# Low parts of the weights on VectorE, paired delta-net products, and the sink attention's value products in one group

## The chip, the cores and the metric

One core of one Trainium2 chip runs the whole program. The metric is the time of one execution on the device in microseconds (us); the figure for a kernel is the median of its runs. TensorE (PE in the profile) multiplies matrices, VectorE (DVE), ScalarE (ACT) and GpSimd (POOL) do the elementwise work, and SyncE (SP) issues the DMAs.

## The reference

Two layers of a bidirectional encoder over 512 tokens of width 1024, all in float32. What matters of a layer:

```
h = rms_norm(x); split(h @ w_in) -> na q,k,v | swa q,k,v | delta net q,k,v,z,beta,a | gates
y_na  = neighborhood_attention_2d(...)       # 4 heads, softmax over a window
y_swa = sliding_window_gqa(..., sink)        # 8 q heads, 2 kv heads, 128-token blocks
y_gdn = gated_deltanet_bidir(...)            # 4 heads, both directions, chunks of 64
  lower = tril(k_beta @ k.T * decay, -1);  u, w = solve(lower + I, ...)
  per chunk:  v_new = u - w @ S;  S = S * d + k_tail.T @ v_new
merged = sum_i sigmoid(gate_i) * (y_i @ w_branch_i);  x = x + merged @ w_out
h = rms_norm(x); u = conv3(h @ w_up) + b;  x = x + (silu(a) * b) @ w_down
```

## The kernel before

Features lie on the 128 partitions and the 512 tokens along the free dimension, so an activation is eight tiles of 128x512. A dense product of 1024 inputs into 128 outputs is one *chunk* of weights, 128 chunks a layer, numbered by the constants at the head of the file: 0 to 51 feed the three mixers and their gates, 52 to 59 (`CH_OUT`) the output projection, 60 to 103 (`CH_UP`) the up projection, 104 to 127 (`CH_DN`) the down projection. `load_w` fetches a chunk in halves of 128x512. For each half it rounds the weights on ScalarE (line 142, the tile `hi`) and subtracts the rounded from the raw on GpSimd (line 144, the tile `lo`, the low parts). Three buffers each hold `raw`, `hi` and `lo`. `mm3` makes a product from three: high weights with high and with low activations (lines 150, 151), low weights with high activations (line 152).

Inside a layer the order of the steps is in the string `ORDER`: projections and attentions of the sliding window (`sp`, `sa`) and of the neighbourhood (`np`, `na`), then the delta net: gates, projections, `gdn_cross` (`gx`), `gdn_z`, `gdn_solve` (`gs`), `gdn_mid`, `gdn_scan` (`gc`), `gdn_out`, and the merges `mn`, `ms`, `mg`. This is only the order in which the program writes its instructions. When it is built, a scheduler orders each engine's list by a simulated timeline and by the tiles' buffers, so that dense products of later steps stand between the small ones of the delta net and of the attentions. On the chip each engine goes through its list in order. `tc.issue_after(i)` puts an order edge behind instruction `i` for what the block writes on the same engine.

`swa_attend` goes over two pairs of heads and four token blocks of 128. A block has two or three key blocks: for each, four transposes of the probabilities (line 531) into a bank `pt`, a copy to SBUF on ScalarE (tile `th`, through line 80) and, for both kv heads, a product with v (line 535) into halves of 64 columns of the bank `py`. A float32 product is two instructions in the profile.

`gdn_cross` makes, head by head, the decays and the masked products k·k and q·k of the chunks. A head's k and q lie on partitions 0 to 63 or 64 to 127 (`rr`), so its products (line 677) use 64 rows of the array. `gdn_solve` inverts the triangular matrices on VectorE in 31 steps (lines 713 and 715). `gdn_scan` goes over eight chunks in both directions at once: direction `d` uses the 64x64 tile of the array at (64d, 64d), with four heads each, for the products with the state (line 832) and for the state's update (line 843). `gdn_mid` has products of the same shape in which the two tiles alternate (line 812).

Of the kernel before, what the change touches and what calls it, by code (L numbers as in the profile page):

```python
# [61 lines left out]
def encoder_kernel(ctx, tc, xT, wall, par, cst, nab, out, depth=2, dbg=None):  # L62
# [70 lines left out]
    def load_w(l, c, nk=8):  # L133
        if (l, c) in early:
            return early.pop((l, c))
        ws = []
        for o in range(0, nk, 4):
            n = min(4, nk - o)
            raw = wp.tile([128, 4, 128], F32, tag="raw", name=nm("wr"), bufs=NB["raw"])
            lastw[0] = nc.sync.dma_start(out=raw[:, :n], in_=wall[l, c, :, o * 128:(o + n) * 128].rearrange("p (k m) -> p k m", k=n))  # L140
            hi = wp.tile([128, 4, 128], F32R, tag="hi", name=nm("wh"), bufs=NB["hi"])
            S.activation(out=hi[:, :n], in_=raw[:, :n], func=AF.Copy)  # L142
            lo = wp.tile([128, 4, 128], F32R, tag="lo", name=nm("wl"), bufs=NB["lo"])
            G.tensor_tensor(lo[:, :n], raw[:, :n], hi.bitcast(F32)[:, :n], op=ALU.subtract)  # L144
            ws += [(hi[:, k], lo[:, k]) for k in range(n)]
        return ws

# [88 lines left out]
    def n8(a):  # L236
        return a.rearrange("p (n i) -> p n i", n=8)
# [37 lines left out]
    for l in range(depth):  # L275
# [215 lines left out]
        def swa_attend():  # L491
            line[0] = "a"

            y["s"] = [None] * 4
            for ep in range(2):
                yh, yl = (big(F32R, (128, 2, 512), name=n) for n in ("ysh", "ysl"))
                for e in range(2):
                    y["s"][2 * ep + e] = (yh[:, e], yl[:, e])
                for b in range(4):
                    kb0, kb1 = max(0, b - 1), min(4, b + 2)  # L500
                    w = 128 * (kb1 - kb0)
                    pr_ = [None] * 4
                    for e in range(2):
                        c0 = 8 * b + 4 * ep + 2 * e
                        mx, sk = small(2, "s", 8), slice(4 * ep + 2 * e, 4 * ep + 2 * e + 2)
                        for gq in range(2):
                            sc = bank("at")
                            q_, kc = qs[2 * ep + e][gq][:, 128 * b:128 * b + 128], slice(128 * kb0, 128 * kb1)
                            T.matmul(sc[:, 0:w], lhsT=q_, rhs=kdh[gq][:, kc], start=True, stop=False)  # L509
                            T.matmul(sc[:, 0:w], lhsT=q_, rhs=kdl[gq][:, kc], start=False, stop=True)  # L510

                            pr = tmp(name="spr")
                            V.tensor_tensor_reduce(out=pr[:, 0:w], in0=sc[:, 0:w], in1=smask[:, 128 * (b == 0):128 * (b == 0) + w], scale=rqs[:, c0 + gq:c0 + gq + 1],
                                                   scalar=nsink[:, sk.start + gq:sk.start + gq + 1], op0=ALU.add, op1=ALU.min, accum_out=mx[:, gq:gq + 1])
                            pr_[2 * gq + e] = pr
                        es, rs = small(2, "s", 8), small(2, "s", 8)
                        V.tensor_tensor(es, mx, P[:, P_SK + sk.start:P_SK + sk.stop], op=ALU.add)
                        S.activation(out=es, in_=es, func=AF.Exp)
                        for gq in range(2):
                            pr = pr_[2 * gq + e]  # L520
                            S.activation(out=pr[:, 0:w], in_=pr[:, 0:w], func=AF.Exp, bias=mx[:, gq:gq + 1], scale=-1.0, accum_out=rs[:, gq:gq + 1])
                        V.tensor_tensor(rs, rs, es, op=ALU.add)
                        V.reciprocal(rs, rs)
                        for gq in range(2):
                            on("spr", "V").tensor_scalar(pr_[2 * gq + e][:, 0:w], pr_[2 * gq + e][:, 0:w], rs[:, gq:gq + 1], None, op0=ALU.mult)
                    py = bank("at")
                    for kb in range(kb0, kb1):
                        pt = bank("at")
                        c0 = 128 * (kb - kb0)
                        for i in range(4):  # L530
                            T.transpose(pt[:, 128 * i:128 * i + 128], pr_[i][:, c0:c0 + 128], ident)  # L531
                        pT = tmp(name="th")
                        copy("th", pT, pt)
                        for gq in range(2):
                            T.matmul(py[64 * gq:64 * gq + 64, 0:256], lhsT=vst[:, 128 * kb + 64 * gq:128 * kb + 64 * gq + 64],  # L535
                                     rhs=pT[:, 256 * gq:256 * gq + 256], start=kb == kb0, stop=kb == kb1 - 1, tile_position=(0, 64 * gq))
                    bs = slice(128 * b, 128 * b + 128)
                    pyv = py[:, 0:256].rearrange("p (e t) -> p e t", e=2)
                    S.activation(out=yh[:, :, bs], in_=pyv, func=AF.Copy)
                    V.tensor_tensor(yl[:, :, bs], pyv, yh.bitcast(F32)[:, :, bs], op=ALU.subtract)  # L540
# [109 lines left out]
        def gdn_cross():  # L650
# [4 lines left out]
            Xo, Xg, Lt = (big(F32, (128, 32, 32), name=n) for n in ("Xo", "Xg", "Lt"))  # L655
            kds = [[doubled(kq[j][i][:, :, 0, :]) for i in range(2)] for j in range(2)]
            qdec = pair(name="qd") + pair(name="qd")
            for hh in range(4):
                j, rr = hh // 2, slice(64 * (hh % 2), 64 * (hh % 2) + 64)
                pe, pr = decay_sums(hh, (msr, blk))  # L660
                eg = tmp(name="eg")
                S.activation(out=eg, in_=pr, func=AF.Exp)
                for d in range(2):
                    r = slice(64 * d, 64 * d + 64)
                    for i in range(2):
                        ns = slice(4 * i, 4 * i + 4)
                        V.tensor_tensor(n8(qdec[hh])[r, ns], n8(eg)[r, ns], kq[j][i][rr, :, 1, :], op=ALU.mult)  # L667
                T.matmul(pe, lhsT=idb, rhs=nmb.unsqueeze(1).to_broadcast([128, 8, 64]), start=False, stop=True)
                e = tmp(name="E")
                S.activation(out=e, in_=pe, func=AF.Exp)  # L670
                on("ebk", "V").tensor_tensor(n8(e), n8(e), bc(bk, hh, 0, 8), op=ALU.mult)
                xt = tmp(name="X")
                for n0 in (0, 4):
                    kd = kds[j][n0 // 4]
                    pk = bank("gd")
                    for n in range(4):
                        T.matmul(pk[:, 128 * n:128 * n + 128], lhsT=kd[rr, n].rearrange("p d i -> p (d i)"),
                                 rhs=kq[j][n0 // 4][rr, n].rearrange("p c i -> p (c i)"), start=True, stop=True)
                    pkv = pk.rearrange("p (n c i) -> p c n i", n=4, c=2)
                    en = n8(e)[:, n0:n0 + 4]  # L680
                    V.tensor_tensor(n8(xt)[:, n0:n0 + 4], pkv[:, 0], en, op=ALU.mult)
                    V.tensor_tensor(Qu[n0 // 4 * 2 + hh // 2][:, :, hh % 2], pkv[:, 1], en, op=ALU.mult)

                for q4 in range(4):
                    r = slice(32 * q4, 32 * q4 + 32)
                    o = 32 * (q4 % 2)
                    cpx = (S.activation if q4 % 2 else G.tensor_copy)(
                        out=Xg[r].rearrange("p i (h n) -> p h n i", h=4)[:, hh], in_=n8(xt)[r, :, o:o + 32], **({"func": AF.Copy} if q4 % 2 else {}))
                    if q4 == 2:
                        lastg[0] = cpx  # L690
                    if q4 in (0, 3):
                        S.activation(out=Xo[r, 8 * hh:8 * hh + 8], in_=n8(xt)[r, :, 32 - o:64 - o], func=AF.Copy)
            Rt = big(F32, (128, 32, 32), "Rt")

        def gdn_solve():
# [121 lines left out]
        def gdn_scan():  # L817
# [7 lines left out]
            for s in range(8):  # L825
                ns = (s, 7 - s)
                half = [slice(0, 64), slice(64, 128)]
                if s:
                    pv = bank("gd", (128, 4, 64))
                    for d, r in enumerate(half):  # L830
                        for hh in range(4):
                            T.matmul(pv[r, hh], lhsT=n8(wn[hh])[r, ns[d]], rhs=SA(ns[d])[r, hh], start=True, stop=True,  # L832
                                     tile_position=(64 * d, 64 * d))
                    for d, r in enumerate(half):
                        V.tensor_tensor(VN(ns[d])[r], pv[r], VN(ns[d])[r], op=ALU.add)
                if s < 7:
                    pd = bank("gd", (128, 4, 64))
                    sd = tmp(shape=(128, 8, 64), name="sd")[:, 0:4]
                    for d, r in enumerate(half):
                        if s:  # L840
                            G.tensor_tensor(sd[r], SA(ns[d])[r], hn(dec[:, 64:96])[r, :, ns[d]].unsqueeze(2).to_broadcast([64, 4, 64]), op=ALU.mult)
                        for hh in range(4):
                            T.matmul(pd[r, hh], lhsT=kT(ns[d], hh)[r], rhs=VN(ns[d])[r, hh], start=True, stop=True,  # L843
                                     tile_position=(64 * d, 64 * d))
                    for d, r in enumerate(half):
# [286 lines left out]
```

## Time and profile before

| what | value |
|---|---|
| median of 3 runs | 1711.9 us (1708.8 to 1712.89) |
| the profiled execution | 1711.75 us, span 1710.0 us |
| mean granted TensorE clock | 0.986 |
| busy TensorE | 1656.6 us (97%) |
| busy VectorE | 1008.1 us (59%) |
| busy GpSimd | 834.5 us (49%), of it line 144 683.8 us in 512 instructions of 1344 ns |
| busy ScalarE | 739.1 us (43%) |
| the chain that ended last | TensorE 79%, VectorE 14% |

Busy is the union of an engine's instructions; matmuls overlap, so their steps are read from start to start. In the timeline a row may merge neighbouring instructions of one line ("x16"), and the time from its start to the next row's start is what the run takes. The two layers lie at 0 to about 860 us and from there to the end; in each the mixers come first, then the two projections of the feed-forward part.

### The profile page before, as it was taken

To read this page: it belongs to the slowest core of one execution; us is meant where nothing else is said; L and a number is where in the kernel's file an instruction comes from. 1 tells how busy PE (TensorE), PEld (TensorE's weight loads), DVE (VectorE), ACT (ScalarE), POOL (GpSimd) and SP (SyncE) were. 2 spreads that over 40 slices of the span, in tenths; PEclk is the share of its full clock that TensorE was granted. 3 is DMA by queue.
4 is the path that set the end of the run, shared out by engine and by line. 5 is a ranking of instruction groups with operands and counts; after the bars stand their busy time and mean duration, and the time that the engine had idled before them with its cause. 6 is when DMAs were issued, how large, how long until landed. Compare 5 with 4: busy or idle time off the path is not lost.

```text
span 1710.0 us, 25217 instructions
## 1 busy us (share of the span) xinstructions
PE 1656.6 (97%) x9196; PEld 1319.6 (77%) x9196; DVE 1008.1 (59%) x1809; ACT 739.1 (43%) x1436; POOL 834.5 (49%) x752
## 2 busy tenths in 40 slices
PE   7989999999999999999999998899999999999999
PEld 5766767777888888878886776777878888888887
DVE  5489996534547777741125898955255487777200
ACT  5445545423445444443334555554234354444321
POOL 4665442264544555544448554422644545555543
PEclk9989999999999999999999999999999999999999
DMA  5222211122452332234333221110324523222432
GB/s 205 74 64 76 70 62 45 38 69 73 132 190 87 99 99 96 96 115 132 114 104 94 67 72 56 56 44 26 99 91 138 178 87 99 93 93 92 136 121 70
DMA packets 91500, 160.46 MB, mean 94 GB/s; under 512 B 10352, under 2 KB 17136, under 8 KB 91376
## 3 DMA queue, kind: packets, MB, share of 16 engines
q1 hardware_dynamic: 91376, 158.85, 28.9%
q8 instruction: 72, 1.18, 0.3%
q14 instruction: 52, 0.43, 0.1%
HBM read 147.80 MB, written 8.39 MB: 91 GB/s over the span
## 4 chain that ended last, share of the span: by engine, by line
PE 79%; DVE 14%; issue 3%; ACT 2%; DMA 1%; POOL 0%; SPq 0%; DVEq 0%; ACTq 0%; POOLq 0%
PE mm L152 23%; PE mm L150 23%; PE mm L151 23%; DVE Rt L715 1%; DVE Tm L713 1%; PE at L535 1%; PE at L531 1%; DVE qd L667 1%; DVE lg L428 1%; DVE fix L172 1%; PE gd L843 1%; PE gd L832 1%; DVE fix L170 1%; PE gd L812 1%; PE at L509 1%
## 5 line engine op out<-in xcount | busy, mean ns | idle before, releaser
L144 POOL TENSOR_TENSOR wl<-wr,wh 128x512 fp32r<-128x512 f32 (+1 forms) x512 | 683.8, 1344 | 792.2 <-ACT wh L142 739.1
L150 PE MATMUL mm<-hh,wh 128*128 128x512 f32 x1408 | 560.2, 398 | 15.3 <-ACT wh L142 13.1
L152 PE MATMUL mm<-hh,wl 128*128 128x512 f32 x1408 | 559.3, 399 | 1.8 <-POOL wl L144 1.7
L151 PE MATMUL mm<-hl,wh 128*128 128x512 f32 x1408 | 556.0, 395 | 0.1
L142 ACT ACTIVATE wh<-wr 128x512 fp32r<-128x512 f32 (+1 forms) x512 | 312.4, 617 | 354.7 <-PE mm L151 213.0
L150 PEld LDWEIGHTS mm<-hh,wh 128*128 128x128 f32 x1408 | 268.0, 190 | 74.2 <-ACT wh L142 15.9
L152 PEld LDWEIGHTS mm<-hh,wl 128*128 128x128 f32 x1408 | 267.7, 190 | 65.1 <-POOL wl L144 6.2
L151 PEld LDWEIGHTS mm<-hl,wh 128*128 128x128 f32 x1408 | 267.7, 190 | 58.3 <-issue 1.9
L234 DVE SCALAR_TENSOR_TENSOR cv<-up,fix,cv 128x511 f32<-128x511 f32 x88 | 142.0, 1613 | 2.8
L233 DVE SCALAR_TENSOR_TENSOR cv<-up,fix,cv 128x511 f32<-128x511 f32 x88 | 85.9, 977 | 88.5 <-ACT cv L232 88.5
L152 PE MATMUL mm<-act,wl 128*128 128x512 f32 x352 | 137.2, 390 | 0.6 <-POOL wl L144 0.6
L150 PE MATMUL mm<-act,wh 128*128 128x512 f32 x352 | 137.1, 389 | 0.3 <-ACT wh L142 0.3
L151 PE MATMUL mm<-act,wh 128*128 128x512 f32 x352 | 137.0, 389 | 0.0
L971 DVE TENSOR_TENSOR xo<-xo,mm 128x512 f32<-128x512 f32 x16 | 11.0, 687 | 192.3 <-PE mm L152 192.3
L232 ACT ACTIVATE cv<-up,fix 128x512 f32<-128x512 f32 x88 | 70.8, 809 | 34.7 <-DVE up L280 34.7
L162 ACT ACTIVATE act<-cv 128x512 fp32r<-128x512 f32 x44 | 27.8, 632 | 126.0 <-DVE cv L954 126.0
L152 PEld LDWEIGHTS mm<-act,wl 128*128 128x128 f32 x352 | 66.1, 188 | 15.3 <-POOL wl L144 1.3
L150 PEld LDWEIGHTS mm<-act,wh 128*128 128x128 f32 x352 | 66.1, 188 | 14.2 <-ACT wh L142 0.7
L151 PEld LDWEIGHTS mm<-act,wh 128*128 128x128 f32 x352 | 66.1, 188 | 13.7
L953 ACT ACTIVATE cv<-cv 128x512 f32<-128x512 f32 x44 | 27.8, 633 | 86.2 <-DVE cv L234 86.2
L280 DVE TENSOR_TENSOR up<-mm,rstd 128x512 f32<-128x512 f32 x88 | 59.5, 680 | 8.2 <-ACT rstd L228 8.2
L900 ACT ACTIVATE gt<-gt 128x512 f32<-128x512 f32 x48 | 30.2, 630 | 66.4 <-DVE gt L280 66.3
(285 smaller groups left out, 2228.5 us busy)
## 6 DMA issues: line engine op xcount, KB each, us to landing
wr<-in_wall_dram SPq DMA_DIRECT2D x496, 256.0 KB, 2.8
xs<-xo SPq DMA_DIRECT2D x24, 256.0 KB, 2.9
xo<-xs SPq DMA_DIRECT2D x24, 256.0 KB, 3.7
xo<-in_xT_dram SPq DMA_DIRECT2D x16, 256.0 KB, 4.9
sw<-raw SPq DMA_DIRECT2D x40, 64.0 KB, 2.0
wr<-in_wall_dram SPq DMA_DIRECT2D x16, 128.0 KB, 3.3
out_dram<-xo SPq DMA_DIRECT2D x8, 256.0 KB, 2.1
nab<-in_nab_dram SPq DMA_DIRECT2D x8, 248.0 KB, 2.8
```

Source lines behind the costliest of these rows:

```text
L142: S.activation(out=hi[:, :n], in_=raw[:, :n], func=AF.Copy)
L144: G.tensor_tensor(lo[:, :n], raw[:, :n], hi.bitcast(F32)[:, :n], op=ALU.subtract)
L150: T.matmul(acc, lhsT=wh, rhs=rh, start=start, stop=False)
L151: T.matmul(acc, lhsT=wh, rhs=rl, start=False, stop=False)
L152: T.matmul(acc, lhsT=wl, rhs=rh, start=False, stop=stop)
L162: S.activation(out=hi, in_=src, func=AF.Copy)
L232: S.activation(out=dst, in_=src, func=AF.Identity, scale=w[:, 1:2], bias=bias)
L233: V.scalar_tensor_tensor(dst[:, 1:L], src[:, 0:L - 1], w[:, 0:1], dst[:, 1:L], op0=ALU.mult, op1=ALU.add)
L234: V.scalar_tensor_tensor(dst[:, 0:L - 1], src[:, 1:L], w[:, 2:3], dst[:, 0:L - 1], op0=ALU.mult, op1=ALU.add)
L280: V.tensor_tensor(dst, acc, rstd, op=ALU.mult)
L900: S.activation(out=gt[q], in_=gt[q], func=AF.Tanh, scale=0.5)
L953: S.activation(out=cv[0], in_=cv[0], func=AF.Silu)
```

## The change

Four edits. In `load_w` the subtraction for chunks below `CH_UP` goes to VectorE; those of the up and down projections stay on GpSimd. In `gdn_cross` two heads are worked together: first the decays of both, then for each half of the chunks the products of both, one after the other from rows 0 to 63 and 64 to 127, into two banks. In `gdn_scan` the loops over heads and directions change places for the products, so that the two tiles alternate. In `swa_attend` all transposes of a token block come first, and the products with v of all its key blocks are written behind them, with an order edge behind the last transpose.

```diff
-            G.tensor_tensor(lo[:, :n], raw[:, :n], hi.bitcast(F32)[:, :n], op=ALU.subtract)
+            (G if c >= CH_UP else V).tensor_tensor(lo[:, :n], raw[:, :n], hi.bitcast(F32)[:, :n], op=ALU.subtract)
...
                     py = bank("at")
+
+                    pTs = []
                     for kb in range(kb0, kb1):
                         pt = bank("at")
                         c0 = 128 * (kb - kb0)
                         for i in range(4):
-                            T.transpose(pt[:, 128 * i:128 * i + 128], pr_[i][:, c0:c0 + 128], ident)
+                            lt = T.transpose(pt[:, 128 * i:128 * i + 128], pr_[i][:, c0:c0 + 128], ident)
                         pT = tmp(name="th")
                         copy("th", pT, pt)
-                        for gq in range(2):
-                            T.matmul(py[64 * gq:64 * gq + 64, 0:256], lhsT=vst[:, 128 * kb + 64 * gq:128 * kb + 64 * gq + 64],
-                                     rhs=pT[:, 256 * gq:256 * gq + 256], start=kb == kb0, stop=kb == kb1 - 1, tile_position=(0, 64 * gq))
+                        pTs.append(pT)
+                    with tc.issue_after(lt.ins):
+                        for kb, pT in zip(range(kb0, kb1), pTs):
+                            for gq in range(2):
+                                T.matmul(py[64 * gq:64 * gq + 64, 0:256], lhsT=vst[:, 128 * kb + 64 * gq:128 * kb + 64 * gq + 64],
+                                         rhs=pT[:, 256 * gq:256 * gq + 256], start=kb == kb0, stop=kb == kb1 - 1, tile_position=(0, 64 * gq))
...
-            for hh in range(4):
-                j, rr = hh // 2, slice(64 * (hh % 2), 64 * (hh % 2) + 64)
-                pe, pr = decay_sums(hh, (msr, blk))
...
+            for j in range(2):
+                es, xts = [], []
+                for e in range(2):
+                    hh, rr = 2 * j + e, slice(64 * e, 64 * e + 64)
+                    pe, pr = decay_sums(hh, (msr, blk))
...
                 for n0 in (0, 4):
                     kd = kds[j][n0 // 4]
-                    pk = bank("gd")
+                    pks = [bank("gd") for _ in range(2)]
                     for n in range(4):
-                        T.matmul(pk[:, 128 * n:128 * n + 128], lhsT=kd[rr, n].rearrange("p d i -> p (d i)"),
-                                 rhs=kq[j][n0 // 4][rr, n].rearrange("p c i -> p (c i)"), start=True, stop=True)
...
+                        for e in range(2):
+                            rr = slice(64 * e, 64 * e + 64)
+                            T.matmul(pks[e][:, 128 * n:128 * n + 128], lhsT=kd[rr, n].rearrange("p d i -> p (d i)"),
+                                     rhs=kq[j][n0 // 4][rr, n].rearrange("p c i -> p (c i)"), start=True, stop=True)
+                    for e in range(2):
+                        pkv = pks[e].rearrange("p (n c i) -> p c n i", n=4, c=2)
+                        en = n8(es[e])[:, n0:n0 + 4]
+                        V.tensor_tensor(n8(xts[e])[:, n0:n0 + 4], pkv[:, 0], en, op=ALU.mult)
+                        V.tensor_tensor(Qu[n0 // 4 * 2 + j][:, :, e], pkv[:, 1], en, op=ALU.mult)
...
-                    for d, r in enumerate(half):
-                        for hh in range(4):
+                    for hh in range(4):
+                        for d, r in enumerate(half):
                             T.matmul(pv[r, hh], lhsT=n8(wn[hh])[r, ns[d]], rhs=SA(ns[d])[r, hh], start=True, stop=True,
                                      tile_position=(64 * d, 64 * d))
...
-                        for hh in range(4):
+                    for hh in range(4):
+                        for d, r in enumerate(half):
                             T.matmul(pd[r, hh], lhsT=kT(ns[d], hh)[r], rhs=VN(ns[d])[r, hh], start=True, stop=True,
                                      tile_position=(64 * d, 64 * d))
```

## Rows read from the trace of the kernel before

**Rows 1.** The page, busy tenths of 40 slices of 42.75 us, PE is TensorE, DVE is VectorE.

```profile
PE   7989999999999999999999998899999999999999
...
DVE  5489996534547777741125898955255487777200
```

**Rows 2.** Busy us by engine and instructions in four stretches, then granted clock and DMA.

```profile
90.00:270.00 180.00, 162.95 (x960) 123.90 (x958) 160.24 (x373) 95.27 (x219) 90.64 (x123) 0.93 0.21 65
270.00:430.00 160.00, 159.35 (x1358) 123.90 (x1357) 78.70 (x201) 62.11 (x140) 63.20 (x57) 1.00 0.18 59
930.00:1110.00 180.00, 164.45 (x966) 125.54 (x965) 163.23 (x378) 95.60 (x219) 96.16 (x123) 0.96 0.20 65
1110.00:1290.00 180.00, 179.65 (x1457) 140.43 (x1457) 87.25 (x218) 70.13 (x157) 71.49 (x62) 0.99 0.21 68
```

**Rows 3.** The same view, line 144 alone, on GpSimd (POOL), in two stretches.

```profile
90.00:270.00 180.00, 51.50 (x39) 0.93 0.21 65
930.00:1110.00 180.00, 53.31 (x38) 0.96 0.20 65
```

**Rows 4.** The timeline of VectorE: start us, us, engine, line, operation, tiles.

```profile
93.06 0.17 DVE L171 SCALAR_TENSOR_TENSOR fix<-fix 128x8 f32<-128x8 f32 x1
93.16 1.26 DVE L170 SCALAR_TENSOR_TENSOR fix<-fix 128x32 f32<-128x32 f32 x1
...
245.47 1.30 DVE L715 TENSOR_TENSOR Rt<-Rt,Tm 128x87 f32<-128x87 f32 x1
...
931.18 1.77 DVE L301 TENSOR_TENSOR raw<-raw,sw 128x512 f32<-128x512 f32 x1
...
1092.86 0.71 DVE L713 TENSOR_TENSOR Tm<-Lt,Rt 128x60 f32<-128x60 f32 x1
```

**Rows 5.** The timeline of GpSimd at the same place.

```profile
93.07 2.51 POOL L144 TENSOR_TENSOR wl<-wr,wh 128x512 fp32r<-128x512 f32 x2
```

**Rows 6.** Line 163 alone: ns minimum, median and maximum, first and last start.

```profile
L163 DVE TENSOR_TENSOR act<-cv,act x44: 677/692/694, 533.1 to 1595.7; 128x512 fp32r<-128x512 f32 x44
```

**Rows 7.** The timeline of TensorE, narrow products of lines 832 and 812 and their neighbours.

```profile
300.04 1.14 PE L812 MATMUL gd<-vtok,W 64*64 64x64 f32 x30
301.11 0.33 PE L803 MATMUL gd<-fix,dup 128*128 128x128 f32 x1
...
308.10 0.56 PE L812 MATMUL gd<-vtok,W 64*64 64x64 f32 x12
308.60 0.44 PE L803 MATMUL gd<-fix,dup 128*128 128x128 f32 x2
...
350.04 0.39 PE L151 MATMUL mm<-ysl,wh 128*128 128x512 f32 x1
350.27 0.39 PE L152 MATMUL mm<-ysh,wl 128*128 128x512 f32 x1
350.59 0.96 PE L832 MATMUL gd<-SA,wn 64*64 64x64 f32 x16
351.48 0.50 PE L150 MATMUL mm<-ysh,wh 128*128 128x512 f32 x1
```

**Rows 8.** The same timeline, products of the sink attention (line 535).

```profile
303.55 0.65 PE L535 MATMUL at<-th,sv 128*64 128x256 f32 x4
304.13 0.65 PE L531 MATMUL at<-fix,spr 128*128 128x128 f32 x4
...
1097.79 1.08 PE L535 MATMUL at<-th,sv 128*64 128x256 f32 x8
1098.80 0.45 PE L509 MATMUL at<-kdh,qs 128*128 128x384 f32 x1
```

**Rows 9.** The same timeline, cross products of the delta net (line 677).

```profile
1010.40 1.16 PE L677 MATMUL gd<-kq,dup 64*128 64x128 f32 x8
1011.49 0.50 PE L150 MATMUL mm<-hh,wh 128*128 128x512 f32 x1
```

**Rows 10.** The waits of TensorE in 90 to 270 us: in total, times, longest.

```profile
PE at L193 <- DVE rb L190: 5.9, 1, 5.9
```

More of the change, by code (lines that the diff above doesn't have):

```diff
@@ L657, in gdn_cross @@
             qdec = pair(name="qd") + pair(name="qd")
-            for hh in range(4):
-                j, rr = hh // 2, slice(64 * (hh % 2), 64 * (hh % 2) + 64)
-                pe, pr = decay_sums(hh, (msr, blk))
[L661 to L672, printed above, removed]
+            for j in range(2):
[3 more added lines that the diff above has]
+                    pe, pr = decay_sums(hh, (msr, blk))
+                    eg = tmp(name="eg")
+                    S.activation(out=eg, in_=pr, func=AF.Exp)
+                    for d in range(2):
+                        r = slice(64 * d, 64 * d + 64)
+                        for i in range(2):
+                            ns = slice(4 * i, 4 * i + 4)
+                            V.tensor_tensor(n8(qdec[hh])[r, ns], n8(eg)[r, ns], kq[j][i][rr, :, 1, :], op=ALU.mult)
+                    T.matmul(pe, lhsT=idb, rhs=nmb.unsqueeze(1).to_broadcast([128, 8, 64]), start=False, stop=True)
+                    ex = tmp(name="E")
+                    S.activation(out=ex, in_=pe, func=AF.Exp)
+                    on("ebk", "V").tensor_tensor(n8(ex), n8(ex), bc(bk, hh, 0, 8), op=ALU.mult)
+                    es.append(ex)
+                    xts.append(tmp(name="X"))
@@ L673, in gdn_cross @@
                 for n0 in (0, 4):
                     kd = kds[j][n0 // 4]
-                    pk = bank("gd")
+                    pks = [bank("gd") for _ in range(2)]
                     for n in range(4):
-                        T.matmul(pk[:, 128 * n:128 * n + 128], lhsT=kd[rr, n].rearrange("p d i -> p (d i)"),
-                                 rhs=kq[j][n0 // 4][rr, n].rearrange("p c i -> p (c i)"), start=True, stop=True)
-                    pkv = pk.rearrange("p (n c i) -> p c n i", n=4, c=2)
@@ L680, in gdn_cross @@
[L680 to L692, printed above, removed]
+                        for e in range(2):
+                            rr = slice(64 * e, 64 * e + 64)
+                            T.matmul(pks[e][:, 128 * n:128 * n + 128], lhsT=kd[rr, n].rearrange("p d i -> p (d i)"),
+                                     rhs=kq[j][n0 // 4][rr, n].rearrange("p c i -> p (c i)"), start=True, stop=True)
@@ new lines, in gdn_cross @@
+                    for e in range(2):
[3 more added lines that the diff above has]
+                        V.tensor_tensor(Qu[n0 // 4 * 2 + j][:, :, e], pkv[:, 1], en, op=ALU.mult)
+                for e in range(2):
+                    hh = 2 * j + e
+                    for q4 in range(4):
+                        r = slice(32 * q4, 32 * q4 + 32)
+                        o = 32 * (q4 % 2)
+                        cpx = (S.activation if q4 % 2 else G.tensor_copy)(
+                            out=Xg[r].rearrange("p i (h n) -> p h n i", h=4)[:, hh], in_=n8(xts[e])[r, :, o:o + 32], **({"func": AF.Copy} if q4 % 2 else {}))
+                        if q4 == 2:
+                            lastg[0] = cpx
+                        if q4 in (0, 3):
+                            S.activation(out=Xo[r, 8 * hh:8 * hh + 8], in_=n8(xts[e])[r, :, 32 - o:64 - o], func=AF.Copy)
```

## The prediction

> **What bounds the kernel now.** I began with the engine table and the slices of the page [rows 1]: TensorE (PE) is at nine tenths or more in all but four slices, and VectorE (DVE) reaches nine only in the fourth to sixth, the 24th and the 26th. So the layer's mixer has two kinds of stage, and I cut windows to part them [rows 2]. In 90 to 270 us (layer 0) and 930 to 1110 us (layer 1) VectorE works 160.2 and 163.2 of 180 us while TensorE works 163.0 and 164.5, at a granted clock of 0.93 and 0.96 (stretches at 1.2 GHz after it idled, the rest at 2.4). TensorE idles 17.0 and 15.5 us there. Its longest wait is 5.9 us, for a VectorE instruction at the end of a chain of tiny ones [rows 10]. These stages hold the neighbourhood attention, the delta net's projections, `gdn_cross` and `gdn_solve`. From 270 to 430 and from 1110 to 1290 TensorE works 159.4 of 160 and 179.7 of 180 us, and VectorE half of that. There, what leaves TensorE's list shortens the run; in the first kind, what leaves VectorE's.
>
> **The low parts.** Line 144 runs 512 times. Chunks below 60 are 60 a layer with two halves each, so 120 a layer, 240 in all, go from GpSimd (POOL) to VectorE; the 272 of the up and down projections stay. Of the 120, 39 and 38 lie in the two VectorE-bound stages [rows 3]. The price of one on VectorE is that of line 163, the same subtraction with the same shapes: 0.69 us [rows 6]. That adds 39 x 0.69 = 26.9 and 38 x 0.69 = 26.2 us.
>
> What does it take away? A `scalar_tensor_tensor` on 128x8 takes 0.17 us at 93.06. The one on 128x32 at 93.16 takes 1.26 us: at 93.07 GpSimd starts two subtractions that take 2.51 us, so the first ends where this one does, about 94.4 [rows 4, 5]. VectorE is held until GpSimd's instruction is over. I counted, in each stage, the VectorE instructions that lie over a line-144 subtraction and take at least 0.1 us more than the shortest of their own line and shape: 30 from 93.16 to 245.47, with 26.9 us too much in all, and 32 from 931.18 to 1092.86, with 29.1 us [rows 4]. If every hold goes, VectorE gains 26.9 and pays 26.9 in layer 0, and gains 29.1 for 26.2 in layer 1: even. The bounds are 27 us a layer dearer (no hold was on its chain) and 3 us cheaper. I take zero, since the stage is VectorE's and holds and subtractions stand in the same list.
>
> The rest, about 81 a layer, cost 81 x 0.69 = 56 us of VectorE in the stages where it works half the time. Taken at nothing: TensorE's full list hides them. Without that cover they would be 56 us a layer.
>
> The move adds a wait. VectorE now waits in line 144 for ScalarE's rounding in line 142, and that waits for a free buffer or the weight transfer. Behind it stands all other VectorE work, and for that wait the softmax, the solve and the evacuation of the banks. The raw buffer is freed after this read too, so a late subtraction makes the next weight transfer on SP's queue late. No DMA is moved.
>
> **The scan.** In `gdn_scan` four products of one 64x64 tile now alternate with four of the other. Today a run of 16 goes from 350.59 to 351.48, 0.89 us [rows 7]. Products of the same shape that already alternate (line 812) need 0.50 us for 12 (308.10 to 308.60) and 1.07 us for 30 (300.04 to 301.11): 0.57 / 18 = 0.032 us each, so 0.50 + 4 x 0.032 = 0.63 us for 16. That is 0.26 us less. There are 7 runs each for lines 832 and 843 in a layer, 28 in all: 28 x 0.26 = 7.3 us, nearly all in TensorE's full stage. VectorE's first half starts at most 0.2 us later, which the dense work around it hides.
>
> **The sink attention.** A run of four products takes 0.58 us (303.55 to 304.13), one of eight 1.01 us (1097.79 to 1098.80) [rows 8]. Joining two runs saves 2 x 0.58 - 1.01 = 0.15 us, and one entry into the narrow tiling: from a dense product to the first narrow one there are 0.32 us (350.27 to 350.59) [rows 7] against the dense step of 0.23, so 0.09. Together 0.24 us. The 40 key blocks would become 16 runs: 24 joints, 24 x 0.24 = 5.8 us at most, and nothing if dense work still parts them. The new edge orders the products only behind the transposes; the last block's evacuation on ScalarE comes after that, so in blocks of three I expect one joint of two. I take half, 2.9 us. Products of the first key block come later, but the output of the block needs the last one anyway.
>
> **The delta net's cross products.** Both heads of a pair now alternate between rows 0 to 63 and 64 to 127. Today eight same-row products take 1.09 us (1010.40 to 1011.49) [rows 9], about 0.11 apart inside a run. No row shows two row halves side by side. The bounds are nothing, and two for the price of one: 64 pairs x 0.11 = 7.0 us. The alternating 64x64 tiles [rows 7] are the nearest rows, and they lie at the upper end. But this work is in VectorE's stage, where a shorter TensorE list partly becomes idle time, so half counts: 3.5 us. The banks suffice: two of three are used at a time, after the decay sums are read. VectorE's instructions are the same number; the pair's masks come first and the products of both heads behind them, so GpSimd's first copy of a pair comes some VectorE instructions later, the second sooner. I leave that at nothing.
>
> **Sum.** 7.3 + 2.9 + 3.5 + 0 = 13.7 us. The profiled execution took 1711.75 us (span 1710.0), the median is 1711.9, so they are one basis: 1711.9 - 13.7 = 1698.
>
> **Rivals.** *Holds were worth more.* TensorE's 32.5 us of idle time and the reduced clock, 180 x 0.07 + 180 x 0.04 = 20 us, hang on VectorE's chains; a held instruction delays a whole chain, such as the one before the 5.9 us wait, whereas a subtraction of 0.69 us may be put where nobody waits. If a third of these 52 us returns, another 17: 1681. Against it: the subtractions stand in the same full list.
>
> *VectorE's list becomes longer* (the other side). The holds go, but were partly slack, and the subtractions arrive in full. What is left of GpSimd's work in the stage (90.6 - 51.5 = 39.1 of 180 us) [rows 2, 3] can hold the new subtractions as it held others: 39 x 39.1 / 180 x 0.65 = 5.5 us a layer. With no relief that is 27 + 5.5 = 32 us a layer against 20 us in which VectorE idles now; if half of those are usable, 22 a layer, 44 in all, less the scan and the sink's 10.2: +34, so 1746. With half the relief it is 27 + 5.5 - 14 - 10 = 8.5 a layer, 17 less 10: +7, 1719. It decides from some 6 us a layer upward. For it: VectorE's tight 89 and 91%, and the new wait for line 142. Against it: the count above.
>
> The Trainium skill ("SBUF — State Buffer", section "Who interferes with whom") says that VectorE and GpSimd share one port pair, and that of a GpSimd instruction that reads SBUF and a VectorE instruction with two SBUF inputs the second to start stands still until the first has finished. The trace agrees: the 128x32 instruction at 93.16 took 1.26 us beside GpSimd's [rows 4, 5]. By that rule the subtraction, with two SBUF inputs, keeps the conflict with GpSimd's other work, and the 1719 of the rival would be the outcome rather than 1698.
>
> *It doesn't do what it says.* Dense work parts the products, row halves do not overlap, and the scan's gain is met by a few us a layer of VectorE: 1711.9 - 7.3 + 6 = 1711.
>
> **How the numbers follow.** Forecast case (1690 to 1706) 0.50; holds worth more 0.16; unchanged 0.14; VectorE longer 0.20. About 5 us (0.3%) is what a measurement here can tell from no change. The forecast case and the first rival are faster: 0.66. The third is within 0.3%: 0.14. The second rival is slower: 0.20. The range leaves out the better part of the 1746 and the deepest part of the first rival, together some 0.2: 1677 to 1722. The forecast's own range is 1690 to 1706.
>
> **What would show it.** The scan's runs of 16 at 0.6 us; sink products in runs of 8 and 12, lines 832, 843 and 535 with a smaller busy time on TensorE; cross products in runs with two starts per 0.11 us; small VectorE instructions back at 0.17 us beside a busy time of VectorE some 100 us higher (240 x 0.69 less some 60 of holds); GpSimd at about half. Wrong it would be if the stage from 90 us on were over 6 us longer than 180, with TensorE waiting in line 152 for VectorE's low parts, or if VectorE waited in front of line 144 for ScalarE.

## The result and the profile after

The changed kernel takes 1685.3 us (median of 4, 1682.5 to 1685.65) against 1712.4 (1708.8 to 1715.77) for the kernel before, beside it on one chip: a ratio of 0.984 [0.982, 0.986], 27 us less. The forecast of 1698 had the sign right and half of the size. 1685 is inside the range and outside the forecast case's own 1690 to 1706, and it came by a term that the sum had put at zero, as the experiments show.

The page of the changed kernel, in its span, engine table, two rows of slices and three groups (busy us and mean ns, then idle time ahead and what ended it):

```profile
span 1683.8 us, 25142 instructions
...
PE 1640.5 (97%) x9196; PEld 1311.3 (78%) x9196; DVE 1061.0 (63%) x2049; ACT 737.8 (44%) x1436; POOL 529.7 (31%) x512
...
PE   7999999999999999999999998999999999999999
...
DVE  5599895746648777741147888867566577777200
...
PE 87%; DVE 7%; issue 3%; POOL 1%; ACT 1%; DMA 1%; SPq 0%; POOLq 0%; DVEq 0%; ACTq 0%
...
L152 PE MATMUL mm<-hh,wl 128*128 128x512 f32 x1408 | 560.3, 398 | 7.2 <-DVE wl L144 7.2
...
L144 POOL TENSOR_TENSOR wl<-wr,wh 128x512 fp32r<-128x512 f32 (+1 forms) x272 | 363.0, 1344 | 544.9 <-ACT wh L142 527.6
...
L144 DVE TENSOR_TENSOR wl<-wr,wh 128x512 fp32r<-128x512 f32 x240 | 172.9, 724 | 72.9 <-ACT wh L142 66.3
```

TensorE is now below nine tenths in two slices, not four [rows 1]. VectorE took over 240 subtractions of 0.72 us, 172.9 us in all, yet its busy time rose by only 52.9 us (1008.1 to 1061.0). Its share of the chain that ended last fell from 14% to 7%, and TensorE's rose from 79% to 87%. The same four stretches as in [rows 2], and ahead of them 60 to 110 us (busy us by engine and instructions, TensorE first, VectorE third, GpSimd fifth; then granted clock and DMA):

```profile
60.00:110.00 50.00, 47.50 (x292) 36.29 (x291) 42.25 (x92) 26.50 (x54) 23.68 (x17) 1.00 0.29 85
90.00:270.00 180.00, 173.40 (x1159) 134.56 (x1157) 161.47 (x445) 103.64 (x240) 42.87 (x84) 0.98 0.22 69
270.00:430.00 160.00, 154.28 (x1221) 119.58 (x1222) 96.71 (x228) 59.94 (x130) 22.27 (x22) 0.99 0.19 62
930.00:1110.00 180.00, 172.86 (x1136) 134.62 (x1137) 154.01 (x406) 98.60 (x222) 31.44 (x75) 0.94 0.20 64
1110.00:1290.00 180.00, 175.26 (x1309) 138.06 (x1304) 110.90 (x257) 69.70 (x157) 21.10 (x20) 0.99 0.24 76
```

This is the view to read most closely. From 90 to 270 us VectorE is as busy as before (161.5 against 160.2 us), but it finished 445 instructions in that time, not 373, and TensorE 1159 matmuls, not 960. So much of the busy time before was standing still. The gain is in both layers: VectorE's first read of an up projection's bank (line 280) starts at 503.0 us in layer 0, against 520.7 before, 17.7 us earlier; in layer 1 at 1338.9 against 1365.9, 27.0 earlier. Much of it is there at the very front. The same view of the kernel before, 60 to 110 us:

```profile
60.00:110.00 50.00, 42.27 (x235) 31.01 (x234) 38.54 (x72) 24.32 (x48) 38.72 (x30) 0.90 0.28 84
```

In these 50 us the changed kernel makes 57 more matmuls, about 13 us of work if all were dense at some 0.23 us, and the granted clock is 1.00 where it was 0.90. The first tile of the delta net's `kq` follows: it starts at 108.3 us against 119.4.

What stood there before is the 5.9 us wait of [rows 10]. TensorE's timeline of the kernel before, at that place:

```profile
93.67 0.40 PE L151 MATMUL mm<-hl,wh 128*128 128x512 f32 x1
100.01 1.09 PE L193 MATMUL at<-fix,rb 128*128 128x128 f32 x4 [5.95 <-DVE rb L190]
...
104.57 0.63 PE L152 MATMUL mm<-hh,wl 128*128 128x512 f32 x1
104.99 0.63 PE L150 MATMUL mm<-hh,wh 128*128 128x512 f32 x1
...
105.72 0.40 PE L152 MATMUL mm<-hh,wl 128*128 128x512 f32 x1
105.96 0.40 PE L150 MATMUL mm<-hh,wh 128*128 128x512 f32 x1
```

TensorE idles until line 190 has written `rb`, and then still runs at its lower level, 1.2 GHz (granted clock 0.50 in 100 to 103 us): dense products start 0.42 us apart at 104.57, and 0.24 apart only from 105.72 on. VectorE, which is late here, spends its time on a chain of tiny instructions (lines 170 to 172, a reciprocal square root in steps). Between 85 and 99.5 us seven of them take 1.21 to 1.33 us in place of 0.17. Three of the seven lie beside line 144 (at 85.05, 93.16 and 94.34, the second in [rows 4, 5]), four beside GpSimd's lines 377, 299 and 485, which the change leaves where they are. GpSimd's timeline of the kernel before, just ahead of [rows 5], and the end of VectorE's chain:

```profile
86.28 2.64 POOL L377 TENSOR_TENSOR nqs<-qn,nqs 64x512 fp32r<-64x512 f32 x2
89.01 1.29 POOL L299 TENSOR_TENSOR raw<-raw,fix 128x512 f32<-128x512 f32 x1
90.37 2.62 POOL L485 TENSOR_TENSOR qs<-raw,qs 64x512 fp32r<-64x512 f32 x2
...
99.44 0.43 DVE L190 TENSOR_SCALAR rb<-fix 128x512 f32<-128x512 f32 x1
```

The low parts stood in GpSimd's list behind these lines: counted in the order of the lists, two halves of weights that ScalarE had rounded by 84.2 and 88.5 us were subtracted only from 93.07 us on. VectorE's timeline of the changed kernel, same chain, behind one line of GpSimd's:

```profile
92.13 4.86 POOL L485 TENSOR_TENSOR qs<-raw,qs 64x512 fp32r<-64x512 f32 x3
...
93.77 0.72 DVE L144 TENSOR_TENSOR wl<-wr,wh 128x512 fp32r<-128x512 f32 x1
...
94.48 1.19 DVE L168 TENSOR_SCALAR fix<-fix 128x32 int32<-128x32 int32 x1
...
95.74 1.30 DVE L170 SCALAR_TENSOR_TENSOR fix<-fix 128x32 f32<-128x32 f32 x1
96.97 0.16 DVE L168 TENSOR_SCALAR fix<-fix 128x8 int32<-128x8 int32 x1
97.08 0.19 DVE L171 SCALAR_TENSOR_TENSOR fix<-fix 128x32 f32<-128x32 f32 x1
97.19 0.16 DVE L170 SCALAR_TENSOR_TENSOR fix<-fix 128x8 f32<-128x8 f32 x1
...
100.83 0.42 DVE L190 TENSOR_SCALAR rb<-fix 128x512 f32<-128x512 f32 x1
```

Beside line 485's subtractions VectorE is still held (at 94.48 and 95.74); from 96.97 on the small instructions run at 0.1 us a step. TensorE's waits in 90 to 270 us, and its product with `rb` in the timeline:

```profile
PE mm L152 <- DVE wl L144: 2.5, 1, 2.5
...
PE at L193 <- DVE rb L190: 0.6, 1, 0.6
...
101.30 0.65 PE L193 MATMUL at<-fix,rb 128*128 128x128 f32 x4 [0.61 <-DVE rb L190]
```

The wait for `rb` fell from 5.9 to 0.6 us, but `rb` came no sooner: line 190 starts at 100.83 us, against 99.44 before (99.25 in e1, the run with edit 1 alone). What changed is how much is done by then. VectorE has started 144 instructions ahead of it, not 104, and TensorE's list has 326 dense products ahead of the product with `rb`, not 280, 46 x 0.23 = 10.6 us more work. The scheduler, which orders the lists by its simulated timeline, built other lists for the moved subtractions. So the change of order belongs to edit 1 beside the holds. The wait that the edit added, for a low part on VectorE, is there, with 2.5 us.

Holds counted as in the prediction (VectorE instructions that start during a GpSimd subtraction and take at least 0.1 us more than the shortest of their line and shape): the 240 subtractions that the change moves held 111 VectorE instructions for 94 us before, and none after. Those of the up and down projections, which were not moved, held 139 for 102 us before and 139 for 105 us after.

### The profile page after: what moved, and what is told of

Read it like the earlier page. It is cut to its first block, busy times and chain, and to the rows that moved or that the text cites. A ratio compares the mean times of both kernels' runs of the same rounds, so it can differ in the third digit from the quotient of the medians.

```text
span 1683.8 us, 25142 instructions
## 1 busy us (share of the span) xinstructions
PE 1640.5 (97%) x9196; PEld 1311.3 (78%) x9196; DVE 1061.0 (63%) x2049; ACT 737.8 (44%) x1436; POOL 529.7 (31%) x512
## 4 chain that ended last, share of the span: by engine, by line
PE 87%; DVE 7%; issue 3%; POOL 1%; ACT 1%; DMA 1%; SPq 0%; POOLq 0%; DVEq 0%; ACTq 0%
PE mm L152 26%; PE mm L150 26%; PE mm L151 26%; PE at L533 1%; PE at L540 1%; DVE wl L144 1%; PE at L509 1%; PE gd L688 1%; POOL wl L144 1%; PE gd L826 0%; PE at L438 0%; PE gd L763 0%; DVE spr L513 0%; PE gd L858 0%; DMA xo<-in_xT_dram 0%
## 5 line engine op out<-in xcount | busy, mean ns | idle before, releaser
L144 POOL TENSOR_TENSOR wl<-wr,wh 128x512 fp32r<-128x512 f32 (+1 forms) x272 | 363.0, 1344 | 544.9 <-ACT wh L142 527.6
L144 DVE TENSOR_TENSOR wl<-wr,wh 128x512 fp32r<-128x512 f32 x240 | 172.9, 724 | 72.9 <-ACT wh L142 66.3
L415 POOL TENSOR_SCALAR nab<-nab,fix 128x248 f32<-128x248 f32 (+2 forms) x32 | 34.9, 1104 | 122.2 <-DVE fix L397 50.8
L855 POOL TENSOR_TENSOR sd<-SA,fix 64x256 f32<-64x256 f32 x24 | 16.1, 671 | 165.5 <-DVE SA L865 69.8
```

What stands on the lines that cost most here:

```text
L144: (G if c >= CH_UP else V).tensor_tensor(lo[:, :n], raw[:, :n], hi.bitcast(F32)[:, :n], op=ALU.subtract)
L415: on("nab", "G").tensor_scalar(bias[:, e, 0:w], bias[:, e, 0:w], irn[:, c0:c0 + 1], None, op0=ALU.mult)
```

## The experiments

Three theories stood against each other. **Chains**: a hold delays a dependent chain that TensorE waits for, while a subtraction on VectorE mostly fills a gap, so edit 1 brings most of the gain. **TensorE's list**: the three reordered products bring more than the 13.7 us, and edit 1 is even, as forecast. **Queue and latency**: edit 1 gains not by the holds but because the low part is ready sooner (0.72 us, not 1.34), or because GpSimd's other work no longer queues behind subtractions. That edit 1 also gives TensorE's list another order, and that low parts no longer queue behind GpSimd's other work, are two more ways in which it could gain; no run was made for either alone. All ratios are to the kernel before on the same chip, with 95% intervals.

### One edit alone, and the change without one

e1 makes the edit of line 144 alone, as in the change's diff, and leaves the other three functions as before.

> The kernel before with the low parts of chunks below 60 on VectorE, nothing else. Holds theory (VectorE no longer stands still beside GpSimd's subtractions, so the chains of the front stage of each layer end earlier): 12 to 20 us faster than before, about 1696, the first kq tile of layer 0 at about 108 us instead of 119. TensorE-list theory (the gain of the whole change is its shorter list of narrow products): within 5 us of before.

1691.5 us, 0.988 [0.986, 0.990]: 20.9 us less (18 to 23), by the term that the prediction had put at zero. TensorE's idle time (span less busy) is 1690.7 - 1654.9 = 35.8 us, against 53.4 before.

e2 takes only `gdn_cross` of the change, e3 only the exchanged loops of `gdn_scan`:

```diff
-                    for d, r in enumerate(half):
-                        for hh in range(4):
+                    for hh in range(4):
+                        for d, r in enumerate(half):
```

> The kernel before with the paired cross products of the delta net, nothing else. TensorE-list theory: 4 to 8 us faster, the runs of line 677's products at 59 ns a product. Holds theory: within 4 us of before, for the stage waits on VectorE.

> The kernel before with the alternating products of the scan, nothing else. TensorE-list theory: 7 us faster, runs of 16 in 0.61 us. Waiting theory (the second product of a run waits for VectorE's second half, so what alternation saves is lost in the run): within 3 us of before, several runs of 16 in over 0.9 us.

e2: 1713.7 us, 1.001 [1.000, 1.002], so nothing or a microsecond worse, though the runs of cross products in it take 14.64 us in all against 17.85. TensorE's busy time did not fall (1657.1 us against 1656.6). e3: 1706.9, 0.997 [0.996, 0.999], 5.5 us less; its runs of these products take 19.7 us in all against 25.85, 6.2 less. TensorE's timeline of e3 has the forecast figure, 0.61 us from the first of 16 to the dense product behind:

```profile
358.85 0.68 PE L832 MATMUL gd<-SA,wn 64*64 64x64 f32 x16
359.46 0.50 PE L150 MATMUL mm<-hh,wh 128*128 128x512 f32 x1
```

e4 is the change with `swa_attend` as before.

> The changed kernel with the sink attention as before (products with v behind each key block's transposes). TensorE-list theory: 3 to 6 us slower than the changed kernel, about 1690. Holds theory: within 3 us of the changed kernel's 1685.

1684.4 us, 0.984 [0.983, 0.986], as the whole change: the sink edit is worth nothing that can be measured.

### Holds put back, and GpSimd kept busy without them

e5 and e6 are e1 with extra work for GpSimd behind each moved subtraction. In e5 GpSimd makes the same subtraction once more, into a raw tile that nobody reads afterwards; in e6 it fills that tile twice (a fill writes, so the words "writes and reads nothing" below hold for the reading alone). Both keep the raw buffer longer.

```diff
+            if c < CH_UP:
+                G.tensor_tensor(raw[:, :n], raw[:, :n], hi.bitcast(F32)[:, :n], op=ALU.subtract)
```

```diff
+            if c < CH_UP:
+                for _ in range(2):
+                    G.memset(raw[:, :n], 0.0)
```

> The low parts on VectorE, and behind each GpSimd subtracts the same two tiles again into the raw buffer, which nobody reads after. Holds theory: GpSimd's reading instructions hold VectorE again while its own subtractions stay, so the gain of 20.9 us is lost, 1708 to 1725. Queue theory (the gain is that GpSimd's list is shorter): lost as well, about 1710. Latency theory (a low part is ready 0.6 us sooner on VectorE): 1691, as with the low parts alone.

> The low parts on VectorE, and behind each GpSimd fills the raw buffer twice with zeros: its list is about as long as before, but it writes and reads nothing. Holds theory: within 6 us of the low parts alone, 1688 to 1697. Queue theory: 1705 or more. Latency theory: 1691.

e5: 1739.0 us, 1.015 [1.013, 1.017], slower than the kernel before and above what any of the theories gave. It lies 47.5 us above e1, which ran on another chip; with each taken against its own kernel before (25.0 above, 20.9 below) it is 46. The low part comes from VectorE as in e1, and TensorE's list is nearly e1's at the front (the same for its first 300 products, 330 dense ones ahead of the one with `rb`, 326 in e1), so neither an earlier low part nor the new order makes the gain by itself. That they have no part in it is not shown. The same chain in VectorE's timeline of e5 (line numbers are two higher):

```profile
96.53 1.24 DVE L174 SCALAR_TENSOR_TENSOR fix<-fix 128x32 f32<-128x32 f32 x1
...
98.03 0.98 DVE L172 SCALAR_TENSOR_TENSOR fix<-fix 128x8 f32<-128x8 f32 x1
...
99.26 1.01 DVE L172 SCALAR_TENSOR_TENSOR fix<-fix 128x32 f32<-128x32 f32 x1
100.20 1.30 DVE L173 SCALAR_TENSOR_TENSOR fix<-fix 128x8 f32<-128x8 f32 x1
...
101.51 0.18 DVE L173 SCALAR_TENSOR_TENSOR fix<-fix 128x32 f32<-128x32 f32 x1
```

Instructions of 0.17 us are back at 1 to 1.3. The new line 146 holds 154 VectorE instructions for 127 us.

e6: 1702.1 us, 0.993 [0.991, 0.995], between the figures of the two theories. It is 10.6 above e1, or 9 with each against its own kernel before. It was meant to keep GpSimd's list full without a hold, and is not clean: the fills held 44 VectorE instructions for 18 us. Lines of both engines in its timeline:

```profile
112.72 1.16 DVE L81 CAST nkh<-kn 64x512 fp32r<-64x512 f32 x2
112.86 0.74 POOL L147 MEMSET wr<- 128x512 f32 x1 [1.41 <-PE at L186]
```

Two casts, 0.41 us each by themselves, take 1.16. The fills are 255.5 us of GpSimd's time, where e5's repeats are 340.8; in that proportion the 9 to 10.6 us become 12 to 14, with the cost of the fills' own holds in them. So by this estimate a full GpSimd list, with the raw buffer kept longer, makes up some 14 of e5's 46 us at most. Holds and queue are parted that far and no further.

### How much of it has to move

e7 is edit 1 and the scan, nothing else. e8 is e7 with four more groups of subtractions, products and sums moved from GpSimd to VectorE:

```diff
-ENG = {}
+ENG = {"ql": "V", "nql": "V", "cos": "V", "ma1": "V"}
```

> Low parts on VectorE and the alternating scan, without the paired cross products and with the sink attention as before. If the parts add up as measured alone (20.9 and 5.5 us): 1686, within 3 us of the whole change. If cross or sink help only together with them: 1688 or more.

> As the one before, and the other subtractions and products of the mixers on GpSimd (lines 299, 377, 485 and 914 of the kernel before) go to VectorE too. Holds theory: their holds in the mixers with the low parts alone on VectorE are 23.5 us over both layers, their own work on VectorE 50 instructions of 0.65 us, 33 us: no gain to a few us slower, 1683 to 1694. Queue theory: some us faster.

e7: 1682.3 us, 0.982 [0.980, 0.983], 31.7 us under its kernel before. That is more than 20.9 and 5.5 together. e8: 1692.0, 0.987 [0.985, 0.989], some 10 us worse and not faster as the queue theory had it, although the 11.7 us of holds that line 485 on GpSimd still made in the changed kernel are gone. Here the work costs more on VectorE than the holds did.

e9 is the kernel before with one line changed: only the first 20 chunks of a layer, the mixers' inputs, have their low parts on VectorE, 80 in place of 240.

```diff
-            G.tensor_tensor(lo[:, :n], raw[:, :n], hi.bitcast(F32)[:, :n], op=ALU.subtract)
+            (V if c < CH_MG[0] else G).tensor_tensor(lo[:, :n], raw[:, :n], hi.bitcast(F32)[:, :n], op=ALU.subtract)
```

e10 is the change without edit 1, e11 the change once more, e12 edit 1 and the scan (e7) once more, all on e9's chip.

> The low parts on VectorE for chunks below 20 alone (the projections of the mixers, 40 of 120 a layer); the gates, branches and the output projection stay on GpSimd. Early-chain theory (the holds that cost are those in the chains before the delta net's projections): 14 to 21 us faster than before, about 1696. Proportion theory (every hold removed counts alike): a third to a half of the 20.9 us, 1702 to 1706.

> The whole change without its first edit: low parts on GpSimd as before. Holds theory, with the parts adding up as measured alone: the scan's 5.5 us, 1706 to 1709. TensorE-list theory: 13.7 us faster than before, 1699.

> The whole change once more, beside the next kernel on the same chip: 1685.

> Low parts and scan without cross and sink once more: 1682, if cross and sink cost some 2 to 3 us; 1685 if they do nothing.

| kernel | median us (lowest to highest) | ratio |
|---|---|---|
| e9, 80 low parts alone | 1686.9 (1685.3 to 1687.2) | 0.985 [0.984, 0.987] |
| e10, change without edit 1 | 1711.0 (1708.5 to 1717.0) | 1.000 [0.999, 1.001] |
| e11, change | 1684.9 (1684.4 to 1686.8) | 0.985 [0.983, 0.986] |
| e12, edit 1 and scan | 1681.0 (1680.2 to 1682.8) | 0.983 [0.981, 0.984] |

Two things follow. Without edit 1 the other three edits together bring nothing, where the expectation was the scan's 5.5 us: TensorE's busy time is 1649.1 us in e10, 7.5 less than before, and its idle time 1709.8 - 1649.1 = 60.7, 7.3 more. The wait that costs most is still there, as TensorE's waits of e10 in 90 to 280 us show:

```profile
PE at L193 <- DVE rb L190: 5.4, 1, 5.4
```

And a third of edit 1 brings all of it: e9 lies 24.4 us under the kernel before. The 160 low parts that stay on GpSimd still hold 57 VectorE instructions for 47 us, but later ones, and that costs nothing that can be measured here. Its first `kq` starts at 108.2 us, as in the change (108.3); in e10 it starts at 119.1. The new order goes with it: e9 has 326 dense products ahead of the one with `rb`, e10 has 280, as before.

e12 is the fastest version found. On this chip all its times (up to 1682.8) lie under all of the change's (from 1684.4), 4 us at the median, though the two intervals against the kernel before overlap. e4, with the paired cross products but the sink as before, is by its ratio as slow as the change, so it seems to be the pairing that costs these us. e9's line with the scan's edit was not tried.

## Why the prediction was right and wrong

**The low parts, "I take zero": this step failed.** The counts held. 240 subtractions moved, at 0.72 us (forecast 0.69), and every hold by them in the mixers went. What failed is the sentence that holds and subtractions "stand in the same list" and so weigh the same. Shown: edit 1 alone gives -20.9 us (e1), taking it out of the change gives back 26.1 (e10 against e11), GpSimd's reads put back beside it cost 46 (e5). An estimate from these: e5's 127 us of holds cost at most 46 us and, if its longer GpSimd list cost the 14 of e6, at least 32, so 0.25 to 0.36 us for one. At that rate the 94 us that the change removed were worth 24 to 34. The measured gain is 20.9, so some 173 us of subtractions on VectorE cost only 3 to 13, under 0.1 us for one: a us of hold weighed some five times as much as a us of subtraction, or more. This is a rough mean, and it is uneven: the 47 us of holds left in e9 cost nothing that can be measured. Where the gain comes in is in the trace: VectorE and TensorE get through more work ahead of the product with `rb`, where TensorE waited before (5.9 us, then dense steps of 0.42 us until 105.7). How the missing holds, the low parts' way past GpSimd's other work and the new order of the lists share in it is argued, not shown; only three of the seven long steps of that chain lay beside line 144. The first rival, "holds were worth more", named holds ahead of that wait; its 17 us more are near the 20.9 of edit 1, but its 1681 counted on the other three edits for 13.7. I gave it 0.16, because VectorE was 89 and 91% busy. That busy time was itself full of holds, so it was no evidence against the rival. The bound on this term was wrong too: 3 us a layer at best, where some 10 came.

**The sum.** That the time fell inside the range, on the faster side, is in part luck: the three terms that made up the 13.7 us bring nothing together without edit 1 (e10, 1.000; the scan alone 5.5 us), and the term that was put at zero brought most of the 27.

**"VectorE's list becomes longer".** It did not decide: the new wait for VectorE's low part is 2.5 us in 90 to 270 us. But its mechanism is real further on: e8 moved more work and lost 10 us. The moved subtractions are held in their turn by what GpSimd kept: median 0.685 us, mean 0.724, the longest 1.79, so 240 x 0.039 = 9.4 us in all, close to the 11 of the rival; the 15 that took over 0.76 us all lie beside one of GpSimd's instructions. The Trainium skill's rule ("SBUF — State Buffer", section "Who interferes with whom") is thus borne out by these holds and by e5's, but the 1719 that the prediction drew from it was not: edit 1 gained more than these holds cost.

**The scan, 7.3 us.** Right in mechanism and near in size by itself: 5.5 us of time and 6.2 us of runs (e3). With the low parts on VectorE it is worth more: e7 and e12, which add it to edit 1, lie 31.7 and 30.3 us under their kernels before, e1 20.9, so 9 to 11 us. Not all of its runs are short there. TensorE's timeline of the changed kernel, with the sink's and the cross products' runs below:

```profile
317.79 1.09 PE L858 MATMUL gd<-VN,kT 64*64 64x64 f32 x16
318.81 0.65 PE L540 MATMUL at<-th,sv 128*64 128x256 f32 x4
319.39 0.39 PE L509 MATMUL at<-kdh,qs 128*128 128x256 f32 x1
319.62 0.28 PE L510 MATMUL at<-kdl,qs 128*128 128x256 f32 x1
319.82 0.65 PE L540 MATMUL at<-th,sv 128*64 128x256 f32 x4
...
341.37 0.68 PE L846 MATMUL gd<-SA,wn 64*64 64x64 f32 x16
341.98 0.50 PE L151 MATMUL mm<-hl,wh 128*128 128x512 f32 x1
...
1000.32 1.16 PE L688 MATMUL gd<-kq,dup 64*128 64x128 f32 x8
1001.40 0.50 PE L152 MATMUL mm<-hh,wl 128*128 128x512 f32 x1
...
1007.79 1.16 PE L688 MATMUL gd<-kq,dup 64*128 64x128 f32 x16
1008.88 0.50 PE L151 MATMUL mm<-hl,wh 128*128 128x512 f32 x1
```

A clean run of 16 takes 0.61 us (341.37 to 341.98; forecast 0.63). The run at 317.79 takes 1.02: with the loops exchanged, its first pairs need both halves of VectorE's work, and it stands 0.3 us inside for the second half, which the prediction had put at "at most 0.2 us later, hidden". All runs together, with such waits, take 25.57 us in the change and 27.89 in e7. That is about the 25.85 before, but in e1, with the low parts moved and the old loops, they take 32.96, with waits for VectorE in them and some at the lower clock (0.50 in 328.5 to 332.8 us). Why the gain beside edit 1 is larger than the 5 us between e1's runs and e7's is not shown.

**The sink, 2.9 us.** Measured nothing (e4). The term counted on 12 of the 24 joints, and 8 came: there are 31 runs, down from 39, not 16. A run of 12 exists (243.61 to 245.06), but at 318.81 four, two others, four follow one another as before, with the next block's scores (lines 509 and 510) between them. The runs take 21.94 us, against 25.89 in e4, and that does not reach the end. The order edge lets the products come late, it doesn't bring them together.

**The cross products, 3.5 us.** The bound that no row showed is settled, at its upper end: two row halves do overlap, 16 products in 1.09 us (1007.79) beside 8 in 1.08 (1000.32), and e2 has 22 in 1.75, in TensorE's timeline:

```profile
1029.10 1.83 PE L683 MATMUL gd<-kq,dup 64*128 64x128 f32 x22
1030.85 0.50 PE L151 MATMUL mm<-hl,wh 128*128 128x512 f32 x1
```

The runs shrank from 17.85 us to 13.58 in the change and 14.64 in e2, not the 7 us of full pairing, since the scheduled order leaves some runs without a partner. Of the 3.2 us that e2 saved there, none reached the end: it is VectorE's stage, and "half counts" was too much.

**What would show it.** Scan runs at 0.6 us: in part. Sink runs of 8 and 12: some. Two starts per 0.11 us: in part. Small instructions back at 0.17 us: yes. VectorE some 100 us busier: 53, since 94 us of holds went and not 60, and since neighbours in its timeline overlap by some 0.08 us (the one at 97.08 ends at 97.27, the next starts at 97.19). GpSimd at 529.7 us is 31% of the span, lower than "about half". The signs of being wrong: TensorE does wait in line 152 for VectorE's low parts (2.5 us in one wait, 7.2 in the whole run), but the stage became shorter, not 6 us longer. VectorE does wait in front of line 144 for ScalarE, 66.3 us in all by the page, and the kernel is faster all the same, so that sign was badly chosen.

**Still open.** How the gain of edit 1 divides between the holds, GpSimd's shorter list and the new order of the lists. By the estimate from e6 GpSimd's list has some 14 us at most. For the order no run exists: it would take the lists of the kernel before with the subtractions moved, or the lists of e1 with them on GpSimd. Why e12 is faster than the whole change is argued, not shown: the pair order in `gdn_cross` puts the instructions of two heads together in VectorE's stage, and e2, alone, gains nothing either.

## What to carry to other kernels

Price a hold between two engines on the chain where it falls, not as busy time: count which held instructions stand ahead of a wait of the bounding engine, and distrust a "90% busy" that contains the holds. Then move only the work that collides with that chain; 80 of 240 subtractions gave all of the gain of the 240 here, and e8, which moved other work too, lost. Before the end of a wait is called the cause, see whether the awaited thing came sooner, or whether the list in front of it has changed: moving work to another engine made the scheduler order all lists anew. A shorter list on TensorE in a stage that waits for VectorE becomes idle time, and a reordering of loops or an order edge is a wish to the scheduler until the runs in the trace show that the instructions meet.

## What the runs showed of the hardware

GpSimd fills, which read nothing, held VectorE's casts and products with a scalar: 44 instructions for 18 us in e6, as the two casts in 1.16 us beside a fill of 0.74. I had looked for holds only between subtractions with two inputs on either side. The Trainium skill ("SBUF — State Buffer", section "Who interferes with whom") does say that casts and `tensor_scalar` can collide with GpSimd when they run in a two-port mode. The run agrees that they collide; in which mode they ran no row shows.

Products of 64 rows, placed in alternating row halves, ran two in the time of one: 16 in 1.09 us against 8 in 1.08.
